# A fused transformer block on one NeuronCore: four rounds of 3, 4, 4 and 5 k tiles in place of 4, 4, 4 and 4, idle products on TensorE ahead of w_mod's last rows, casts ahead of affine halves

## Chip, cores, metric

One core of one Trainium2 chip (trn2). The metric is the device time of one execution in microseconds; a kernel's time is the median of its runs.

## What is computed

The reference is one layer of an adaLN-modulated block on x (256 tokens, 2048 channels) in float32:

```python
c_act = silu(c)
mod = c_act @ w_mod + b_mod                  # 2048 -> 6 * 2048
sh1, sc1, g1, sh2, sc2, g2 = split(mod, 6)
h = rmsnorm(x, norm1_w) * (1.0 + sc1) + sh1
x = x + g1 * mixer(h, ...)   # h @ w_in -> q, k, v, z, x/B/C, dt, gates; attention and SSD; w_out
h = rmsnorm(x, norm2_w) * (1.0 + sc2) + sh2
x = x + g2 * swiglu(h, w_ffn_in, w_ffn_out)
return rmsnorm(x, final_norm_w)
```

What matters here is the beginning: h needs sh1 and sc1, and these need the first 4096 columns of all 2048 rows of w_mod (33.5 MB). Only then can h @ w_in begin.

## The kernel before

**Tiles.** Channels lie on the 128 partitions, so x's 2048 channels are 16 k tiles. A weight chunk is four k tiles by 512 columns (1 MB). Every product is made of float32r pieces: ScalarE casts the chunk to `hi`, VectorE makes `lo = w - hi` (`split_chunk`, L339 and L341, two k tiles at a time), the activations are split in the same way (`split_affine`, L309 to L314), and TensorE sums hi x hi, hi x lo and lo x hi. A chunk of kind `cm1` (q, k, B, C) is 48 products of 256 columns (L389 to L392), one of kind `tm` (v) is 24 of 512 columns (L410 to L412).

**Rounds.** So as not to wait for all of w_mod, the first stage goes in rounds over k tiles (`ROUNDS`, L482). A round (loop at L600) loads, for each of w_mod's 16 row blocks kk, the columns of its k tiles of both sections (shift and scale; `mod_load`, 512 KB), and VectorE adds `row * c_act` into `sums` (L632, L634: one operation of 1024 columns). TensorE sums over the partitions with one-column products (`reduce_to`, L610). Round 0 takes some rows straight on TensorE (`ONPE`: both sections of row 11, one of row 15). Columns of sc1 and sh1 follow (L652 to L656), then the affine step makes `hx`, and round r's part of eleven products against w_in (three q, three k, three v, B, C; `first_chunks`) can run. While a round reduces its rows, the chunks of the round before run between pairs of rows; the last two of them (`TAILCH`) run after the columns are there and cover the affine step. Partial sums are added on VectorE (L498); the first product keeps its banks through all rounds.

**Order.** Each engine runs its instructions in the order of the code. `Stream.run` takes a chunk from the queue, splits the next one (load, cast, lo), lets waiting side tasks do a step, and issues the chunk's products. `mod_task` is the lowest of these tasks: it loads the other columns of w_mod (`wm`, 1 MB, L686), and VectorE reduces them in four operations (L695). It has one step per queue entry at most, and its work alternates between a step with a load and an empty one; the chunks of the last round run with a budget that pays for all of it.

**Buffers.** `wraw` has three raw buffers, taken in turn by every chunk and every wm; `wsp` has four of `hi` and four of `lo`, each for two k tiles. `load_chunk`'s DMA is issued on SP, which waits there until the buffer is free; what stands behind it on SP waits too.

**Before the first product.** x is normalized and transposed by TensorE in eight pairs of k tiles (`turn_x`, L471): four pairs early, three behind row 11 (`NEARLY`, L626), the last one behind the first chunk.

Of the kernel before, what the change touches and what calls it, by code (L numbers as in the profile page):

```python
# [152 lines left out]
def tile_hybrid_block(  # L153
# [162 lines left out]

    def load_chunk(ch, parts=1):
        ncol, nk = ch["ncol"], ch["nk"]
        raw = wraw.tile([P, nk, ncol], F32, tag="raw", name=nm("w"), padded_shape=[P, nk, 2048 // nk])
        for k in range(0, nk, nk // parts):  # L320
            r0 = ch["r0"] + k * P
            nc.sync.dma_start(raw[:, k:k + nk // parts, :], ch["w"][
                r0:r0 + nk // parts * P, ch["c0"]:ch["c0"] + ncol].rearrange("(k p) n -> p k n", p=P))
        return raw

    def split_chunk(ch):
        raw = load_chunk(ch)
        got = []
        if ch["kind"] == "dt":

            for k in (0, 8):
# [4 lines left out]
            return got
        for k in range(0, ch["nk"], 2):
            hi = wsp.tile([P, 2, ch["ncol"]], FR, tag="hi", name=nm("hi"), padded_shape=[P, 2, 512])
            A_.copy(hi, raw[:, k:k + 2, :])  # L339
            lo = wsp.tile([P, 2, ch["ncol"]], FR, tag="lo", name=nm("lo"), padded_shape=[P, 2, 512])  # L340
            V.tensor_tensor(lo, raw[:, k:k + 2, :], hi, op=OP.subtract)  # L341
            got += [(hi[:, i, :], lo[:, i, :]) for i in range(2)]
# [161 lines left out]
    def first_chunks(k0, nk):  # L504
        for i, (kind, lst, g, c0) in enumerate(first):
            kept = i < len(kept_banks)
            st.add(dict(kind=kind, w=w_in, r0=k0 * P, c0=c0, k0=k0, nk=nk, first=0 if kept else k0,
                        last=KT - 1 if kept else k0 + nk - 1, act=hact,
                        evacf=add_to(kind, lst, g, 0 if kept else k0), group={}, ncol=512, accs=None,
                        alloc=(lambda i=i: kept_banks[i]) if kept else lambda: [acc() for _ in range(2)],  # L510
                        before=None, after=None, evac=(0.0, 0.0), time=nk / 4))
# [87 lines left out]

    for r, (k0, nk) in enumerate(ROUNDS):  # L600

        nt = nk * P
        sums = modp.tile([P, 2, 512], F32, tag="ma", name=nm("ma"))

        groups = [(misc(), j0, j1, []) for j0, j1 in ([(0, 1), (1, nk)] if r == 0 else [(0, nk)])]

        def reduce_to(group, sec, w, v, stop=False):
            cols, j0, j1, begun = group
            for j in range(j0, j1):
                PE.matmul(cols[:, sec * 4 + j:sec * 4 + j + 1], w[:, j * P:(j + 1) * P], v,  # L610
                          start=not begun, stop=stop, skip_group_check=True)
# [7 lines left out]
        for kk in range(KT):  # L619
            w = mod_load(kk, k0 * P, nt)  # L620
            onpe = ONPE.get(kk, ()) if r == 0 else ()
            for sec in onpe:
                for group in groups:
                    reduce_to(group, sec, w[:, sec, :], cs[:, kk:kk + 1])
            if onpe and kk == min(ONPE):
                for kp in range(NEARLY, KT // 2 - 1):  # L626
                    turn_x(kp, acc)
            rest = [sec for sec in range(2) if sec not in onpe]
            if rest:
                d, w = sums[:, rest[0]:rest[-1] + 1, :nt], w[:, rest[0]:rest[-1] + 1, :]  # L630
                if kk == 0:
                    V.tensor_scalar(d, w, cs[:, kk:kk + 1], None, op0=OP.mult)  # L632
# [16 lines left out]
        for cols, j0, j1, _ in groups:  # L649
            a, b = k0 + j0, k0 + j1  # L650
            if j1 - j0 == 1:
                V.tensor_scalar(sc1[:, a:b], cols[:, 4 + j0:4 + j1], n1T[:, a:b], c1[:, a:b], op0=OP.mult, op1=OP.add)  # L652
            else:
                V.tensor_tensor(sc1[:, a:b], cols[:, 4 + j0:4 + j1], n1T[:, a:b], op=OP.mult)
                V.tensor_tensor(sc1[:, a:b], sc1[:, a:b], c1[:, a:b], op=OP.add)
            V.tensor_tensor(sh1[:, a:b], cols[:, j0:j1], bmT[:, a:b], op=OP.add)  # L656
            for kt in range(a, b):
                split_affine(hx[kt // 2][:, kt % 2, :], xnT[kt // 4][:, kt % 4, :],
                             sc1[:, kt:kt + 1], sh1[:, kt:kt + 1])
                if r == 0:  # L660
                    k = kt - k0
                    if k % 2 == 0:
                        hi, lo = (wsp.tile([P, 2, 512], FR, tag=tag, name=nm(tag)) for tag in ("hi", "lo"))
                    A_.copy(hi[:, k % 2, :], raw[:, k, :])
                    V.tensor_tensor(lo[:, k % 2, :], raw[:, k, :], hi[:, k % 2, :], op=OP.subtract)
# [764 lines left out]
```

## Time and profile before

| | |
|---|---|
| median of 3 runs | 2032.2 us (2031.6 to 2032.31) |
| the profiled execution, device time | 2033.43 us |
| its span in the trace | 2031.7 us |
| granted TensorE clock, mean | 0.996 |
| busy TensorE, VectorE, ScalarE | 98%, 73%, 50% |
| read from HBM | 464.95 MB |

The page gives shares over the whole span. They mix a beginning in which transfers set the pace with a long rest in which TensorE works without a pause, so stretches and single instructions are read beside it. Times within the span count from its start. A transfer's issue and its landing are different things: the issue stands on SP's queue, the landing ends the wait of the engine that needs the data.

### The profile page before, as it was taken

To read this page: it belongs to the slowest core of one execution; us is meant where nothing else is said; L and a number is where in the kernel's file an instruction comes from. 1 tells how busy PE (TensorE), PEld (TensorE's weight loads), DVE (VectorE), ACT (ScalarE), POOL (GpSimd) and SP (SyncE) were. 2 spreads that over 40 slices of the span, in tenths; PEclk is the share of its full clock that TensorE was granted. 3 is DMA by queue.
4 is the path that set the end of the run, shared out by engine and by line. 5 is a ranking of instruction groups with operands and counts; after the bars stand their busy time and mean duration, and the time that the engine had idled before them with its cause. 6 is when DMAs were issued, how large, how long until landed. Compare 5 with 4: busy or idle time off the path is not lost.

```text
span 2031.7 us, 29046 instructions
## 1 busy us (share of the span) xinstructions
PE 1989.4 (98%) x11560; PEld 1746.0 (86%) x11560; DVE 1479.8 (73%) x1957; ACT 1005.9 (50%) x1429; POOL 97.3 (5%) x176
## 2 busy tenths in 40 slices
PE   5999999999999999999999999999999999999998
PEld 4899999888888888888888888888888888888886
DVE  6788887887888888876868787777765555555564
ACT  4443435575666665554544344644444334444443
POOL 1000000001020211100000000100000000000000
PEclk9999999999999999999999999999999999999999
DMA  9998684575565656667777768587865555555553
GB/s 345 348 321 296 229 272 145 175 239 191 192 230 198 228 199 217 223 233 258 274 243 286 274 241 292 182 291 247 283 219 183 194 199 187 198 197 186 199 193 126
DMA packets 218344, 469.02 MB, mean 231 GB/s; under 512 B 10419, under 2 KB 10607, under 8 KB 218208
## 3 DMA queue, kind: packets, MB, share of 16 engines
q1 hardware_dynamic: 214096, 453.61, 64.9%
q0 software_dynamic: 4112, 13.56, 2.1%
q8 instruction: 90, 1.47, 0.3%
q14 instruction: 46, 0.38, 0.1%
HBM read 464.95 MB, written 2.18 MB: 230 GB/s over the span
## 4 chain that ended last, share of the span: by engine, by line
PE 54%; DVE 1%; DMA 1%; issue 0%; ACT 0%; ACTq 0%; DVEq 0%
PE pa L357 25%; PE pa L361 13%; PE pa L410 5%; PE pa L412 5%; PE pa L411 5%; DMA w<-in_w_ssm_proj_dram 1%; PE pb L701 0%; PE pb L720 0%; DVE lo L341 0%; DVE ma L695 0%; DVE s L1298 0%; ACT hi L339 0%; DVE s L1117 0%; DVE t L444 0%; DVE s L1171 0%
## 5 line engine op out<-in xcount | busy, mean ns | idle before, releaser
L341 DVE TENSOR_TENSOR lo<-w,hi 128x1024 fp32r<-128x1024 f32 x662 | 788.8, 1229 | 369.5 <-ACT hi L339 326.3
L339 ACT CAST hi<-w 128x1024 fp32r<-128x1024 f32 x662 | 666.2, 1048 | 550.4 <-PE pa L357 225.1
L357 PE MATMUL pa<-s,hi 128*128 128x512 f32 x3648 | 881.6, 394 | 2.8 <-DVE s L1298 1.2
L357 PEld LDWEIGHTS pa<-s,hi 128*128 128x128 f32 x3648 | 671.2, 189 | 140.8 <-issue 4.4
L361 PEld LDWEIGHTS pa<-s,lo 128*128 128x128 f32 x3648 | 467.7, 191 | 17.8
L361 PE MATMUL pa<-s,lo 128*128 128x256 f32 x3648 | 473.1, 283 | 0.0
L410 PE MATMUL pa<-hi,s 128*128 128x512 f32 x576 | 225.9, 392 | 0.0
L411 PE MATMUL pa<-lo,s 128*128 128x512 f32 x576 | 224.3, 389 | 0.1
L412 PE MATMUL pa<-hi,s 128*128 128x512 f32 x576 | 224.2, 389 | 0.0
L695 DVE SCALAR_TENSOR_TENSOR ma<-wm,cs,ma 128x512 f32<-128x512 f32 x240 | 164.3, 744 | 3.2 <-DMA wm<-in_w_mod_dram 3.2
L443 ACT COPY t<-pa 128x256 f32<-128x256 f32 x160 | 59.6, 372 | 182.9 <-PE pa L361 168.6
L389 PE MATMUL pa<-s,hi 128*128 128x256 f32 x512 | 148.4, 290 | 0.0
L392 PE MATMUL pa<-s,lo 128*128 128x256 f32 x512 | 145.8, 285 | 0.2 <-DVE lo L341 0.2
L391 PE MATMUL pa<-s,hi 128*128 128x256 f32 x512 | 145.6, 284 | 0.0
L410 PEld LDWEIGHTS pa<-hi,s 128*128 128x128 f32 x576 | 108.1, 188 | 23.5 <-ACT s L496 0.6
L411 PEld LDWEIGHTS pa<-lo,s 128*128 128x128 f32 x576 | 108.2, 188 | 23.3 <-DVE lo L341 0.6
L412 PEld LDWEIGHTS pa<-hi,s 128*128 128x128 f32 x576 | 108.1, 188 | 22.8
L389 PEld LDWEIGHTS pa<-s,hi 128*128 128x128 f32 x512 | 99.1, 194 | 2.3 <-ACT s L496 1.3
L391 PEld LDWEIGHTS pa<-s,hi 128*128 128x128 f32 x512 | 99.2, 194 | 1.0 <-issue 1.0
L392 PEld LDWEIGHTS pa<-s,lo 128*128 128x128 f32 x512 | 99.0, 193 | 0.6 <-DVE lo L341 0.6
L444 DVE TENSOR_TENSOR s<-pa,t 128x256 f32<-128x256 f32 x128 | 53.1, 422 | 52.9 <-ACT t L443 48.6
L634 DVE SCALAR_TENSOR_TENSOR ma<-s,cs,ma 128x1024 f32<-128x1024 f32 (+1 forms) x59 | 75.0, 1272 | 2.5 <-DMA s<-in_w_mod_dram 1.1
(243 smaller groups left out, 1119.5 us busy)
## 6 DMA issues: line engine op xcount, KB each, us to landing
w<-in_w_in_dram SPq DMA_DIRECT2D x147, 1024.0 KB, 5.1
w<-in_w_ffn_in_dram SPq DMA_DIRECT2D x88, 1024.0 KB, 5.0
wm<-in_w_mod_dram SPq DMA_DIRECT2D x64, 1024.0 KB, 5.1
w<-in_w_ffn_out_dram SPq DMA_DIRECT2D x44, 1024.0 KB, 5.1
s<-in_w_mod_dram SPq DMA_DIRECT2D x64, 512.0 KB, 10.2
w<-in_w_ssm_proj_dram SPq DMA_DIRECT2D x32, 1024.0 KB, 5.2
w<-in_w_out_dram SPq DMA_DIRECT2D x16, 1024.0 KB, 5.3
s<-acd POOLq DMA_DIRECT2D x16, 512.0 KB, 4.8
```

Source lines behind the costliest of these rows:

```text
L339: A_.copy(hi, raw[:, k:k + 2, :])
L341: V.tensor_tensor(lo, raw[:, k:k + 2, :], hi, op=OP.subtract)
L357: PE.matmul(accs[n], parts[k][0][:, n * P:(n + 1) * P], act(k0 + k), start=(k0 + k == first), stop=False, skip_group_check=True)
L361: PE.matmul(accs[n][:, :S], parts[k][1][:, n * P:(n + 1) * P], act(k0 + k)[:, :S], start=False, stop=(k0 + k == last), skip_group_check=True)
L389: PE.matmul(o, w1, a[:, :S], start=(kk == first and n % 2 == 0), stop=False, skip_group_check=True)
L391: PE.matmul(o, w1, a[:, S:], start=False, stop=False, skip_group_check=True)
L392: PE.matmul(o, w2, a[:, :S], start=False, stop=(kk == last), skip_group_check=True)
L410: PE.matmul(o, xh, hi, start=(kk == first), stop=False)
L411: PE.matmul(o, xh, lo, start=False, stop=False)
L412: PE.matmul(o, xl, hi, start=False, stop=(kk == last))
L634: V.scalar_tensor_tensor(d, w, cs[:, kk:kk + 1], d, op0=OP.mult, op1=OP.add)
L695: V.scalar_tensor_tensor(a[:, i, :], w[:, 2 * k + i, :], cs[:, kk:kk + 1], a[:, i, :], op0=OP.mult, op1=OP.add)
```

## The change

Four things change in the first stage.

1. `ROUNDS` is (0, 3), (3, 4), (7, 4), (11, 5). Round 0 loads 384 columns per section and row, its chunks have three k tiles. The last round has five: the first four as before, the fifth with a tile `w5` (four small loads for four rows), an accumulator `sums5` and one more VectorE operation per row. Its eleven products become 22 queue entries, each a chunk of four k tiles and one of one. A chunk of one k tile takes a whole raw buffer, a whole hi buffer and a whole lo buffer.
2. `ONPE` takes one section of row 11 in place of both.
3. All four remaining transposes stand behind row 11, and behind them six idle products of 128 columns whose result nobody reads (`IDLE`).
4. In round 0 the cast of a k tile stands ahead of its affine half on ScalarE.

```diff
+        per = -(-nk // parts)
+        for k in range(0, nk, per):
+            m = min(per, nk - k)
...
-    NEARLY, ONPE = 4, {11: (0, 1), 15: (1,)}
+    IDLE = 6
+    NEARLY, ONPE = 4, {11: (0,), 15: (1,)}
...
-    ROUNDS = [(0, 4), (4, 4), (8, 4), (12, 4)]
+    ROUNDS = [(0, 3), (3, 4), (7, 4), (11, 5)]
...
-            st.add(dict(kind=kind, w=w_in, r0=k0 * P, c0=c0, k0=k0, nk=nk, first=0 if kept else k0,
+            group = {}
+            for ka in range(k0, k0 + nk, 4):
+                m = min(4, k0 + nk - ka)
+                st.add(dict(kind=kind, w=w_in, r0=ka * P, c0=c0, k0=ka, nk=m, first=0 if kept else k0,
...
-        nt = nk * P
+        nt = min(nk, 4) * P
+        sums5 = t2(2 * P).rearrange("p (a b) -> p a b", a=2) if nk > 4 else None
...
+            if nk > 4 and kk % 4 == 0:
+                w5 = s4(2, 512).rearrange("p a (b c) -> p (a b) c", c=P).rearrange("p (k s) c -> p k s c", k=4)
+                for k in range(4):
+                    nc.sync.dma_start(w5[:, k, :, :], w_mod_s[
+                        (kk + k) * P:(kk + k + 1) * P, 0:2, (k0 + 4) * P:(k0 + 5) * P])
+            if nk > 4:
+                w = w5[:, kk % 4, :, :]
...
+                    V.scalar_tensor_tensor(sums5, w, cs[:, kk:kk + 1], sums5, op0=OP.mult, op1=OP.add)
...
-                for kp in range(NEARLY, KT // 2 - 1):
+                for kp in range(NEARLY, KT // 2):
                     turn_x(kp, acc)
+                idle = misc()
+                for _ in range(IDLE):
+                    PE.matmul(idle[:, :P], ident, ones, start=True, stop=True)
...
-            ch["after"] = lambda: turn_x(KT // 2 - 1)
...
-                split_affine(hx[kt // 2][:, kt % 2, :], xnT[kt // 4][:, kt % 4, :],
-                             sc1[:, kt:kt + 1], sh1[:, kt:kt + 1])
                 if r == 0:
...
                     A_.copy(hi[:, k % 2, :], raw[:, k, :])
+                split_affine(hx[kt // 2][:, kt % 2, :], xnT[kt // 4][:, kt % 4, :],
+                             sc1[:, kt:kt + 1], sh1[:, kt:kt + 1])
```

In the rows of the order below, a name's number is the buffer's; line numbers of the kernel after lie a little higher. TensorE ahead of the first product, before (`s_97` and `s_101` are x, `cs` is c_act, `s_279` row 15 of w_mod, `ma` the sums):

```order
L471 MATMUL pa_264<-ident,s_97 128x128
L471 MATMUL pa_264<-ident,s_101 128x128
L610 MATMUL pb_207<-cs,s_279 128x1
L610 MATMUL pb_208<-cs,s_279 128x1 x3
L610 MATMUL pb_207<-ones,ma_206 128x1 x2
L610 MATMUL pb_208<-ones,ma_206 128x1 x6
L389 MATMUL pa_181<-s_173,hi_303 128x256
```

The same place on TensorE after (`s_288` is row 15):

```order
L475 MATMUL pa_265<-ident,s_97 128x128
L475 MATMUL pa_265<-ident,s_101 128x128
L657 MATMUL pb_271<-ones,ident 128x128 x6
L624 MATMUL pb_207<-cs,s_288 128x1
L624 MATMUL pb_208<-cs,s_288 128x1 x2
L624 MATMUL pb_207<-ones,ma_206 128x1 x2
L624 MATMUL pb_208<-ones,ma_206 128x1 x4
L392 MATMUL pa_181<-s_173,hi_305 128x256
```

Six idle products have come in between the transposes and row 15, and the one-column products are fewer, as the second group has two k tiles instead of three.

VectorE while the last round's rows are reduced, one step, before (`s_2106` and `s_2109` are two rows, `lo` a chunk of the round before):

```order
L634 SCALAR_TENSOR_TENSOR ma_1765<-s_2106,cs,ma_1765 128x1024
L634 SCALAR_TENSOR_TENSOR ma_1765<-s_2109,cs,ma_1765 128x1024
L341 TENSOR_TENSOR lo_2116<-w_2112,hi_2114 128x1024
L341 TENSOR_TENSOR lo_2120<-w_2112,hi_2118 128x1024
L498 TENSOR_TENSOR s_736<-pa_2122,s_736 128x512
L498 TENSOR_TENSOR s_736<-pa_2123,s_736 128x512
```

The same step on VectorE after (`s_1937` is w5, `w_1645` is sums5):

```order
L645 SCALAR_TENSOR_TENSOR w_1645<-s_1937,cs,w_1645 128x256
L664 SCALAR_TENSOR_TENSOR ma_1646<-s_2013,cs,ma_1646 128x1024
L645 SCALAR_TENSOR_TENSOR w_1645<-s_1937,cs,w_1645 128x256
L664 SCALAR_TENSOR_TENSOR ma_1646<-s_2017,cs,ma_1646 128x1024
L344 TENSOR_TENSOR lo_2023<-w_2020,hi_2022 128x1024
L344 TENSOR_TENSOR lo_2027<-w_2020,hi_2026 128x1024
L502 TENSOR_TENSOR s_664<-pa_2030,s_664 128x512
L502 TENSOR_TENSOR s_664<-pa_2031,s_664 128x512
```

Two operations of 256 columns stand in each step more than before.

SP at the beginning of the last round's chunks, before (`w` are chunks, `wm` the loads of `mod_task`):

```order
L322 DMA w_2459<-in_w_in_dram 128x4x512
L686 DMA wm_2469<-in_w_mod_dram 128x2x1024
L322 DMA w_2526<-in_w_in_dram 128x4x512
L322 DMA w_2588<-in_w_in_dram 128x4x512
L686 DMA wm_2598<-in_w_mod_dram 128x2x1024
L322 DMA w_2656<-in_w_in_dram 128x4x512
L322 DMA w_2718<-in_w_in_dram 128x4x512
L686 DMA wm_2728<-in_w_mod_dram 128x2x1024
```

The same place on SP after:

```order
L324 DMA w_2314<-in_w_in_dram 128x4x512
L324 DMA w_2384<-in_w_in_dram 128x512
L720 DMA wm_2390<-in_w_mod_dram 128x2x1024
L324 DMA w_2444<-in_w_in_dram 128x4x512
L324 DMA w_2469<-in_w_in_dram 128x512
L720 DMA wm_2475<-in_w_mod_dram 128x2x1024
L324 DMA w_2531<-in_w_in_dram 128x4x512
L324 DMA w_2555<-in_w_in_dram 128x512
L720 DMA wm_2561<-in_w_mod_dram 128x2x1024
```

One wm used to stand behind every two chunks of four k tiles; now one stands behind every pair of a four-tile and a one-tile chunk, for the first eight pairs.

## Rows read from the trace of the kernel before

**Rows 1.** Page, part 1: busy time of each engine, its share, instructions

```profile
PE 1989.4 (98%) x11560; PEld 1746.0 (86%) x11560; DVE 1479.8 (73%) x1957; ACT 1005.9 (50%) x1429; POOL 97.3 (5%) x176
```

**Rows 2.** Stretches: length, busy PE, PEld, DVE, ACT, POOL; clock, DMA share, GB/s

```profile
0.00:40.00 40.00, 15.01 (x68) 14.09 (x68) 21.29 (x30) 17.10 (x25) 8.12 (x21) 1.00 0.97 334
...
167.00:234.00 67.00, 66.86 (x483) 62.65 (x483) 60.06 (x70) 25.13 (x28) 0.00 (x0) 1.00 0.83 287
234.00:302.00 68.00, 68.00 (x504) 65.17 (x504) 56.63 (x77) 27.98 (x31) 0.00 (x0) 1.00 0.74 251
```

**Rows 3.** Waits of TensorE: total us, times, longest

```profile
PE pb L610 <- DMA s<-in_w_mod_dram: 7.1, 1, 7.1
```

**Rows 4.** Timeline of TensorE to the first chunk's end: start, us, engine, line

```profile
29.37 3.54 PE L610 MATMUL pb<-cs,s 128*128 128x1 f32 x16 [7.14 <-DMA s<-in_w_mod_dram]
32.78 2.80 PE L471 MATMUL pa<-ident,s 128*128 128x128 f32 x12
35.37 1.71 PE L610 MATMUL pb<-cs,s 128*128 128x1 f32 x8
36.94 3.55 PE L610 MATMUL pb<-ones,ma 128*128 128x1 f32 x16
40.35 0.56 PE L389 MATMUL pa<-s,hi 128*128 128x256 f32 x1
...
44.34 0.39 PE L389 MATMUL pa<-s,hi 128*128 128x256 f32 x1
...
47.92 0.28 PE L392 MATMUL pa<-s,lo 128*128 128x256 f32 x1
48.04 0.60 PE L471 MATMUL pb<-ident,s 128*128 128x128 f32 x4
```

**Rows 5.** Transfers, 0 to 120 us, 40 slices of 3 us

```profile
GB/s 18 193 353 327 359 361 386 388 386 388 386 387 386 386 388 384 385 387 386 388 386 387 387 386 387 389 354 258 141 306 320 262 405 388 382 102 366 392 391 382
```

**Rows 6.** Timeline of VectorE ahead of the first product

```profile
37.97 0.28 DVE L652 TENSOR_SCALAR sc<-pb,v,c 128x1 f32<-128x1 f32 x1 [2.48 <-PE pb L610]
...
39.55 0.69 DVE L665 TENSOR_TENSOR lo<-w,hi 128x512 fp32r<-128x512 f32 x1
```

**Rows 7.** Timeline of VectorE while the last round's rows are reduced

```profile
192.40 0.69 DVE L498 TENSOR_TENSOR s<-pa,s 128x512 f32<-128x512 f32 x1 [2.03 <-PE pa L392]
...
204.97 2.60 DVE L634 SCALAR_TENSOR_TENSOR ma<-s,cs,ma 128x1024 f32<-128x1024 f32 x2
...
209.75 1.28 DVE L498 TENSOR_TENSOR s<-pa,s 128x512 f32<-128x512 f32 x2
210.95 2.59 DVE L634 SCALAR_TENSOR_TENSOR ma<-s,cs,ma 128x1024 f32<-128x1024 f32 x2
```

**Rows 8.** Timeline of TensorE at the last step of that stretch

```profile
225.94 0.39 PE L412 MATMUL pa<-hi,s 128*128 128x512 f32 x1
226.17 0.39 PE L410 MATMUL pa<-hi,s 128*128 128x512 f32 x1
226.69 0.50 PE L411 MATMUL pa<-lo,s 128*128 128x512 f32 x1
```

**Rows 9.** Groups of VectorE, 45 to 300 us: busy us, mean ns, idle before

```profile
L313 DVE TENSOR_SCALAR t<-s,sc,sh 128x256 f32<-128x256 f32 x12 | 4.9, 408 | 0.1
```

**Rows 10.** Last round: ScalarE, VectorE, SP in time; median us from issue to landing

```profile
251.80 2.00 ACT L339 CAST hi<-w 128x1024 fp32r<-128x1024 f32 x2
252.88 2.36 DVE L341 TENSOR_TENSOR lo<-w,hi 128x1024 fp32r<-128x1024 f32 x2 [2.11 <-ACT hi L339]
259.96 2.73 DVE L695 SCALAR_TENSOR_TENSOR ma<-wm,cs,ma 128x512 f32<-128x512 f32 x4
263.81 2.35 DVE L341 TENSOR_TENSOR lo<-w,hi 128x1024 fp32r<-128x1024 f32 x2
266.18 5.77 SPq L322 DMA_DIRECT2D w<-in_w_in_dram  x2
...
w<-in_w_in_dram SPq DMA_DIRECT2D x10, 1024.0 KB, 5.0
```

More of the change, by code (lines that the diff above doesn't have):

```diff
@@ L318, in load_chunk @@
         ncol, nk = ch["ncol"], ch["nk"]
-        raw = wraw.tile([P, nk, ncol], F32, tag="raw", name=nm("w"), padded_shape=[P, nk, 2048 // nk])
-        for k in range(0, nk, nk // parts):
+        raw = wraw.tile([P, nk, ncol], F32, tag="raw", name=nm("w"), padded_shape=[P, max(nk, 4), 2048 // max(nk, 4)])
+        per = -(-nk // parts)
+        for k in range(0, nk, per):
+            m = min(per, nk - k)
             r0 = ch["r0"] + k * P
-            nc.sync.dma_start(raw[:, k:k + nk // parts, :], ch["w"][
-                r0:r0 + nk // parts * P, ch["c0"]:ch["c0"] + ncol].rearrange("(k p) n -> p k n", p=P))
+            nc.sync.dma_start(raw[:, k:k + m, :], ch["w"][
+                r0:r0 + m * P, ch["c0"]:ch["c0"] + ncol].rearrange("(k p) n -> p k n", p=P))
         return raw
@@ L337, in split_chunk @@
         for k in range(0, ch["nk"], 2):
[L338 to L342, printed above, removed]
+            m = min(2, ch["nk"] - k)
+            hi, lo = (wsp.tile([P, m, ch["ncol"]], FR, tag=tag, name=nm(tag), padded_shape=[P, m, 1024 // m])
+                      for tag in ("hi", "lo"))
+            A_.copy(hi, raw[:, k:k + m, :])
+            V.tensor_tensor(lo, raw[:, k:k + m, :], hi, op=OP.subtract)
+            got += [(hi[:, i, :], lo[:, i, :]) for i in range(m)]
         return got
@@ L506, in first_chunks @@
             kept = i < len(kept_banks)
-            st.add(dict(kind=kind, w=w_in, r0=k0 * P, c0=c0, k0=k0, nk=nk, first=0 if kept else k0,
[L508 to L511, printed above, removed]
+            group = {}
+            for ka in range(k0, k0 + nk, 4):
+                m = min(4, k0 + nk - ka)
+                st.add(dict(kind=kind, w=w_in, r0=ka * P, c0=c0, k0=ka, nk=m, first=0 if kept else k0,
+                            last=KT - 1 if kept else k0 + nk - 1, act=hact,
+                            evacf=add_to(kind, lst, g, 0 if kept else k0), group=group, ncol=512, accs=None,
+                            alloc=(lambda i=i: kept_banks[i]) if kept else lambda group=group: group.get("accs") or [
+                                acc() for _ in range(2)],
+                            before=None, after=None, evac=(0.0, 0.0), time=m / 4))
     TAILCH, BIASR = 2, 2
@@ L609, in reduce_to @@
             for j in range(j0, j1):
-                PE.matmul(cols[:, sec * 4 + j:sec * 4 + j + 1], w[:, j * P:(j + 1) * P], v,
+                if j == 4:
+                    w, j = sums5[:, sec, :], 0
+                    o = cols[:, 8 + sec:9 + sec]
+                else:
+                    o = cols[:, sec * 4 + j:sec * 4 + j + 1]
+                PE.matmul(o, w[:, j * P:(j + 1) * P], v,
                           start=not begun, stop=stop, skip_group_check=True)
@@ L619, in tile_hybrid_block @@
         for kk in range(KT):
+            if nk > 4 and kk % 4 == 0:
[5 more added lines that the diff above has]
+                w = w5[:, kk % 4, :, :]
+                if kk == 0:
+                    V.tensor_scalar(sums5, w, cs[:, kk:kk + 1], None, op0=OP.mult)
+                else:
+                    V.scalar_tensor_tensor(sums5, w, cs[:, kk:kk + 1], sums5, op0=OP.mult, op1=OP.add)
             w = mod_load(kk, k0 * P, nt)
@@ L648, in tile_hybrid_block @@
                 reduce_to(group, sec, sums[:, sec, :], ones[:, 0:1], True)
[L649 to L652, printed above, removed]
+        ready = [(cols, j0, 4 + j0, k0 + j0, k0 + min(j1, 4)) for cols, j0, j1, _ in groups]
+        if nk > 4:
+            ready.append((groups[0][0], 8, 9, k0 + 4, k0 + 5))
+        for cols, jh, jc, a, b in ready:
+            ps_h, ps_c = cols[:, jh:jh + b - a], cols[:, jc:jc + b - a]
+            if b - a == 1:
+                V.tensor_scalar(sc1[:, a:b], ps_c, n1T[:, a:b], c1[:, a:b], op0=OP.mult, op1=OP.add)
             else:
-                V.tensor_tensor(sc1[:, a:b], cols[:, 4 + j0:4 + j1], n1T[:, a:b], op=OP.mult)
+                V.tensor_tensor(sc1[:, a:b], ps_c, n1T[:, a:b], op=OP.mult)
                 V.tensor_tensor(sc1[:, a:b], sc1[:, a:b], c1[:, a:b], op=OP.add)
-            V.tensor_tensor(sh1[:, a:b], cols[:, j0:j1], bmT[:, a:b], op=OP.add)
+            V.tensor_tensor(sh1[:, a:b], ps_h, bmT[:, a:b], op=OP.add)
             for kt in range(a, b):
-                split_affine(hx[kt // 2][:, kt % 2, :], xnT[kt // 4][:, kt % 4, :],
-                             sc1[:, kt:kt + 1], sh1[:, kt:kt + 1])
                 if r == 0:
@@ L664, in tile_hybrid_block @@
                     A_.copy(hi[:, k % 2, :], raw[:, k, :])
+                split_affine(hx[kt // 2][:, kt % 2, :], xnT[kt // 4][:, kt % 4, :],
+                             sc1[:, kt:kt + 1], sh1[:, kt:kt + 1])
+                if r == 0:
                     V.tensor_tensor(lo[:, k % 2, :], raw[:, k, :], hi[:, k % 2, :], op=OP.subtract)
@@ L668, in tile_hybrid_block @@
             first_chunks(k0, nk)
-        st.run(PHASE0, len(first))
+        st.run(PHASE0, len(first) * -(-nk // 4))
     mods_done = []
@@ L1093, in start_attention @@
             tk[f"att{i}"] = spawn(attention(i), 0)
-    st.queue[-3]["after"] = start_attention
-    for i, k in ((-2, "B"), (-1, "C")):
-        st.queue[i]["after"] = lambda i=i, k=k: start_conv(k, 0, ubc[i])
+    per = -(-ROUNDS[-1][1] // 4)
+    st.queue[-1 - 2 * per]["after"] = start_attention
+    for i, k in enumerate("BC"):
+        st.queue[-1 - (1 - i) * per]["after"] = lambda i=i, k=k: start_conv(k, 0, ubc[i])
     st.add(dict(kind="dt", w=w_in, r0=0, c0=DT0, k0=0, nk=KT, first=0, last=KT - 1, act=hact, evacf=dt_evac,
```

## The prediction

> **What bounds the kernel now.** I read the page's engine line first [rows 1]: TensorE is busy for 98% of the span. The stretches [rows 2] place the rest: nearly all of its idle time lies ahead of 40 us, and from there to the end of the four rounds (302 us) it is busy throughout. The list of its waits says the same: the one long wait on a transfer is for w_mod's row 11, 7.1 us [rows 3]. A busy TensorE can still be fed late, since overlapping products hide small gaps, so I then read distances between starts. From 29.37 us TensorE works without a gap through 16 + 12 + 8 + 16 records to the first real product at 40.35 [rows 4]: 52 records in 10.98 us, 0.211 us each. Products keep that slow pace until 44.3; at 47.92 they start 0.12 us apart [rows 4]. Those are the two clock levels, 1.2 and 2.4 GHz. From then on a chunk of four k tiles of q or k costs 48 x 0.12 = 5.76 us, and one of v 24 x 0.23 = 5.46 us (0.2275 each, 225.94 to 226.17 [rows 8]). So two things move the end: when the first chunk is through, and every wait of TensorE that the change creates up to 302 us. Work shifted between rounds moves it not at all, as the products are equally many.
>
> The third view is VectorE in the stretch that reduces the last round's w_mod rows: it is busy 60.1 of 67 us [rows 2]. A step (two rows 2.60, a chunk's lo halves 2.35, two adds 1.28, overlapping) repeats after 210.95 - 204.97 = 5.98 us [rows 7, 10], against TensorE's 5.76. VectorE still waited 2.03 us for TensorE at 192.40 [rows 7]; at 226.17 TensorE's next product starts 0.52 us later instead of 0.23 [rows 8]. The reserve is used up exactly there.
>
> **The change, part by part.** The sum is made against the profiled execution, 2033.4 us, which is 1.2 us over the median of the runs, 2032.2; I put the difference on the median.
>
> *Start.* Round 0's w_mod rows fall from 524 to 393 KB. At the 387 GB/s that the transfers sustain [rows 5] a row takes 1.02 us instead of 1.36; the twelfth row then lands 4.1 us earlier, and TensorE starts at 25.3. Its records are again 52: 6 for row 11, 16 transposes, 12 for six idle products (an fp32 product shows as two records, as L610 does), 6 and 12. At the slow pace the first group's columns are ready after 44 of them, at 34.6. The trace shows one rise of the clock, 4 us after full-width products begin; it does not show whether transposes and idle products bring it. I take a rise near their end, 31.5, which halves the rest: columns at 33.1. From columns to chunk end VectorE decides: first lo 2.4 us later (37.97 to 40.24, [rows 6]), second 2.3 later, third 1.4, and 11 products x 0.12 behind it: 7.4 us, so 40.5. Before, the chunk ended at 48.04, or 46.6 without the 12 products that go to later rounds. Gain 6.1, less 0.5 because the second chunk's lo stands behind two rows (1.6 us of waiting; before 1.2, with transposes that now come early): **-5.6**. Bounds: no rise ahead of the products -3.9; a rise at the first transposes -7.1; if a 1.5 KB piece costs what a 2 KB piece does, about -2. I take -5.6, since 6 us of transposes and idle products stand there in one piece. Casts ahead of affine halves are inside the 2.4; ScalarE has nothing else to do there.
>
> *Round 0.* A step loads two rows and a 0.79 MB chunk, 4.7 us at 387 GB/s; TensorE needs 36 x 0.12 = 4.3 us and 0.3 of bias and vector work. The second chunk's data is there some 6 us ahead, and that lead covers it: nothing. But its last two chunks are shorter, and they hide the four affine tiles: VectorE reaches the first lo half of the last one after 0.2 + 4 x 0.85 + 0.5 + 1.1 = 5.3 us, TensorE after 4.5: **+0.8**. The second round begins with that much less lead: **+0.2**.
>
> *Reducing the last round's rows.* The fifth tile adds one 256-column operation per row. Nothing shows it; the nearest row is the 256-column L313, 0.41 us [rows 9]. A step grows by 0.82, to 6.80. The first two steps' 1.6 us go into the 2.03 us wait, the other six make 4.9, of which 0.3 fits: **+4.6** (3.5 to 5). The four small loads per group only add issues on SP ahead of rows that lie a step ahead.
>
> *Last affine.* A fifth tile puts 1.2 us on VectorE ahead of the last chunk's lo, which has 0.3 us to spare, and four more slow records: **+1.4**.
>
> *Last round.* This is the largest term. Each chunk takes one of three raw buffers, and SP may issue a load only when the lo half that reads the buffer's last content is done: 263.81 + 2.35 = 266.16, issue at 266.18 [rows 10]. Now a round has 22 chunks instead of 11, and the order shows one w_mod load (wm) behind each of the first eight pairs of a four-tile and a one-tile chunk. Three buffers then turn once per pair, so a four-tile load waits for the lo half of the four-tile chunk right before it. The loop is landing 5.0, then from the start of the cast to the end of lo 3.44 (251.80 to 255.24), and 0.1 between [rows 10]: 8.55 us. TensorE needs 60 x 0.12 = 7.2 us a pair (6.8 for v). Before, a buffer turned once in two chunks, 11.5 us, and the same loop was hidden. The second pair's lo is ready 7.5 us after the round's start (TensorE gives its hi buffer back after 42 products, 5.0, then a cast and a lo half follow), seven loops make 59.9, the ninth pair is through 5.2 later: 72.6, against 6 x 7.2 + 3 x 6.8 = 63.6 without waits. **+9.0**, bounds 7 and 11 for loops of 8.3 and 8.9. The wm rows themselves (2.73 a pair) fit, as VectorE has 6.8 us of work in 8.55; the two pairs behind the eighth find buffers earlier.
>
> The Trainium skill, page "DMA: Bandwidth & Descriptors", section "Anatomy of one DMA — SWDGE (gpsimd) path", speaks against this cut: a transfer has a fixed part of about 2.0 us and then bytes / 436 GB/s, so smaller loads do not shorten the loop in proportion. By its fit a 1 MB load would take an estimated 4.4 us, the loop 7.95, the term 4.8 and the time 2038.4. The trace's 5.0 for loads issued by SP decides here.
>
> Sum: -5.6 + 0.8 + 0.2 + 4.6 + 1.4 + 9.0 = **+10.4 us**, 2042.6. Its own bounds, with all terms at one end, are 2038 and 2047.
>
> **Rivals.** *The last round's loop is hidden.* For it: VectorE is idle for 11 of the 68 us from 234 to 302 [rows 2]. Against it: the order leaves no other buffer, and idle time of VectorE does not bring a load earlier. It holds if the loop is under 7.2 us: 9.0 falls away, 2033.6, no change. *Faster: the reserves carry both.* Place: the last reduction and the last round. Were lo halves far enough ahead there that both the 4.9 us and the loop vanish, only the start and the affine terms would stand: 2032.2 - 5.6 + 2.4 = 2029, and 2027.5 with the start's upper bound. It decides from a reserve of 5 us at 192 us; the trace has 2.03 there and none at 226. *The start gives little.* If the smaller pieces land no sooner and the clock rises only with the products, -2 stands for -5.6: 2046.2. For it: no row shows a 1.5 KB piece.
>
> **How the numbers follow.** Forecast 0.72, loop hidden 0.11, faster 0.08, start gives little 0.09. A measurement of this kernel tells about 0.2%, 4 us, from no change, so from 2028.1 to 2036.3 is the same. The forecast and the weak start lie above; a small part of the forecast's low end with the hidden loop lies inside: faster 0.08, same 0.14, slower 0.78. The range 2034 to 2048 takes in the forecast's bounds, the weak start and the upper half of the hidden loop; the faster case and that case's lower half stay out, some 0.15.
>
> **What would show it.** Right: the first chunk of 36 products ends near 40.5 us; VectorE runs without a gap through the last reductions in steps of 6.8; in the last round SP's four-tile loads are 8.5 us apart, each right behind a lo half, and TensorE waits for lo or hi about 1.4 us in each of six or seven pairs; the round's end lies some 10 us later. Wrong: loads issued ahead of the lo half before them, pairs 7.2 us apart, or a step of VectorE below 6.3 us; and for the start, row 11 still landing at 29 us.

## The result and the profile after

The changed kernel takes 2044.37 us (median of 6 runs, 2043.21 to 2045.06), the kernel before 2032.26 us in the same session: ratio 1.0057, 95% interval 1.0046 to 1.0067. It is slower by 12 us where 10.4 were forecast. Of the profiled executions the spans are 2042.3 and 2031.7 us, 10.6 apart; the ledger below is made against these.

Part 1 of the page after, the answer to [rows 1], looks the same as before: TensorE is busy for 98%. The share hides what happened; the stretches and the waits show it. Here are stretches near those of [rows 2] (length, busy PE, PEld, DVE, ACT, POOL, then granted clock, DMA share, GB/s), against 66.86 of 67 and 68.00 of 68 us busy there. They are stretches of time and not of equal work: in the changed kernel the last round's rows are reduced from 145 to 216 us, and its chunks run from 229 us on.

```profile
167.00:234.00 67.00, 63.33 (x446) 58.07 (x445) 61.91 (x86) 21.28 (x24) 0.00 (x0) 1.00 0.72 244
234.00:313.00 79.00, 71.76 (x484) 64.26 (x483) 58.36 (x78) 25.19 (x30) 0.00 (x0) 1.00 0.79 260
```

What TensorE waited for from 229 to 313 us (total us, times, longest), all of it data of its own chunks, where before nothing was listed:

```profile
PE pa L395 <- DVE lo L344: 3.7, 8, 0.8
PE pa L414 <- DVE lo L344: 2.3, 3, 0.8
PE pa L413 <- ACT hi L343: 0.9, 2, 0.5
```

These waits count only the time in which nothing overlaps. The full loss ("lost" below) is the distance between starts of consecutive TensorE records beyond the usual one of the same shape (0.12 us for 256 columns, 0.23 for 512), summed over a stretch that ends at the same piece of work in both traces:

| piece of work | lost before | lost after | difference | forecast |
|---|---|---|---|---|
| start to the second chunk's end (55.02 and 45.60), less 96 and 72 products of 0.12 | 43.5 | 37.0 | -6.5 | -5.6 |
| rest of round 0 | 1.2 | 1.2 | 0.0 | 0 |
| second round's sums, last chunks of round 0, second round (to 166 and 145 us) | 3.3 | 4.8 | +1.5 | +1.0 |
| reduction of the last round's rows (to 232 and 216) | 2.2 | 6.0 | +3.8 | +4.6 |
| last affine step, with four more one-column records (to 245 and 229) | 0.0 | 2.3 | +2.3 | +1.4 |
| last round (to 302 and 313) | 0.0 | 11.8 | +11.7 | +9.0 |
| behind it, to 400 us | | | +0.9 | 0 |
| one stall near 870 us | 3.7 | 0.0 | -3.7 | 0 |
| rest | | | +0.6 | 0 |

The start, TensorE in time (start, us, engine, line), the answer to [rows 4]:

```profile
25.91 1.10 PE L624 MATMUL pb<-cs,s 128*128 128x1 f32 x6 [3.57 <-DVE ma L664]
26.88 3.30 PE L475 MATMUL pa<-ident,s 128*128 128x128 f32 x16
30.01 1.50 PE L657 MATMUL pb<-ones,ident 128*128 128x128 f32 x12
...
31.94 1.48 PE L624 MATMUL pb<-ones,ma 128*128 128x1 f32 x12
33.66 0.39 PE L392 MATMUL pa<-s,hi 128*128 128x256 f32 x1 [0.24 <-ACT s L311]
...
41.34 0.39 PE L395 MATMUL pa<-s,lo 128*128 128x256 f32 x1 [1.42 <-DVE lo L344]
```

Row 11 is used at 25.9 instead of 29.4, the first product starts at 33.66 instead of 40.35. The 12 idle records take 1.34 us (to 31.35), 0.112 each: the clock was at its upper level before they began (granted clock 0.50 from 28 to 29 us, 1.00 from 30 us on). At 41.34 the second chunk waits 1.42 us for its lo half.

VectorE, one step of the last reduction, the answer to [rows 7]:

```profile
192.29 0.47 DVE L645 SCALAR_TENSOR_TENSOR w<-s,cs,w 128x256 f32<-128x256 f32 x1
192.68 1.28 DVE L664 SCALAR_TENSOR_TENSOR ma<-s,cs,ma 128x1024 f32<-128x1024 f32 x1
193.88 0.48 DVE L645 SCALAR_TENSOR_TENSOR w<-s,cs,w 128x256 f32<-128x256 f32 x1
194.27 1.28 DVE L664 SCALAR_TENSOR_TENSOR ma<-s,cs,ma 128x1024 f32<-128x1024 f32 x1
195.47 2.35 DVE L344 TENSOR_TENSOR lo<-w,hi 128x1024 fp32r<-128x1024 f32 x2
197.74 1.28 DVE L502 TENSOR_TENSOR s<-pa,s 128x512 f32<-128x512 f32 x2
198.94 0.48 DVE L645 SCALAR_TENSOR_TENSOR w<-s,cs,w 128x256 f32<-128x256 f32 x1
```

No idle time, and the step repeats after 198.94 - 192.29 = 6.65 us. The fifth tile's operation moves the next start by 0.39 us, not 0.41.

The last round, ScalarE, VectorE and SP in time, the answer to [rows 10]:

```profile
245.75 2.36 DVE L344 TENSOR_TENSOR lo<-w,hi 128x1024 fp32r<-128x1024 f32 x2 [2.91 <-ACT hi L343]
248.14 2.14 SPq L324 DMA_DIRECT2D w<-in_w_in_dram  x2
252.59 0.37 SPq L720 DMA_DIRECT2D wm<-in_w_mod_dram  x1
253.39 2.51 ACT L343 CAST hi<-w 128x1024 fp32r<-128x1024 f32 x3 [6.21 <-DMA w<-in_w_in_dram]
254.48 2.36 DVE L344 TENSOR_TENSOR lo<-w,hi 128x1024 fp32r<-128x1024 f32 x2 [1.91 <-ACT hi L343]
256.87 2.14 SPq L324 DMA_DIRECT2D w<-in_w_in_dram  x2
```

One turn of the loop is seen whole: lo ends at 248.1, SP issues the next four-tile load at 248.14, ScalarE waits 6.21 us and casts at 253.39, lo ends at 256.84, and the next load goes out at 256.87. The loads stand at 238.41, 248.14, 256.87, 265.81, 274.54, 283.46 and 292.11, 8.95 us apart on average, and TensorE needs 7.2.

### The profile page after: what moved, and what is told of

Same layout as the page of the kernel before. It is cut to its first block, busy times and chain, and to the rows that moved or that the text cites. A ratio compares the mean times of both kernels' runs of the same rounds, so it can differ in the third digit from the quotient of the medians.

```text
span 2042.3 us, 29174 instructions
## 1 busy us (share of the span) xinstructions
PE 1991.7 (98%) x11560; PEld 1742.1 (85%) x11560; DVE 1485.2 (73%) x1986; ACT 1007.3 (49%) x1439; POOL 97.9 (5%) x176
## 4 chain that ended last, share of the span: by engine, by line
PE 79%; DVE 5%; DMA 4%; issue 2%; ACT 1%; POOL 1%; SPq 0%; ACTq 0%; DVEq 0%; POOLq 0%
PE pa L360 39%; PE pa L364 20%; PE pa L414 5%; PE pa L415 5%; PE pa L413 5%; DVE lo L344 3%; DMA w<-in_w_in_dram 2%; ACT hi L343 1%; DMA s<-in_w_mod_dram 1%; PE pb L1021 1%; PE pb L735 1%; DMA w<-in_w_ssm_proj_dram 1%; POOL nt L301 0%; PE pb L1039 0%; DVE ma L729 0%
## 5 line engine op out<-in xcount | busy, mean ns | idle before, releaser
L344 DVE TENSOR_TENSOR lo<-w,hi 128x1024 fp32r<-128x1024 f32 (+1 forms) x673 | 791.6, 1213 | 385.7 <-ACT hi L343 338.7
L343 ACT CAST hi<-w 128x1024 fp32r<-128x1024 f32 (+1 forms) x673 | 668.0, 1035 | 593.4 <-PE pa L360 229.2
L395 PEld LDWEIGHTS pa<-s,lo 128*128 128x128 f32 x512 | 98.6, 193 | 10.4 <-DVE lo L344 9.6
L664 DVE SCALAR_TENSOR_TENSOR ma<-s,cs,ma 128x1024 f32<-128x1024 f32 (+2 forms) x60 | 72.1, 1201 | 1.1
```

What stands on the lines that cost most here:

```text
L343: A_.copy(hi, raw[:, k:k + m, :])
L344: V.tensor_tensor(lo, raw[:, k:k + m, :], hi, op=OP.subtract)
L395: PE.matmul(o, w2, a[:, :S], start=False, stop=(kk == last), skip_group_check=True)
```

## Experiments

Each kernel was timed in turn with the kernel before, which took 2032.6 to 2033.1 us in these sessions and 2032.3 us beside the changed kernel. The ratios are against the kernel before; a difference to the changed kernel goes across sessions and is good to about 0.8 us.

### One-tile chunks out of the raw buffers

```diff
-        raw = wraw.tile([P, nk, ncol], F32, tag="raw", ...)
+        raw = s4(1, 512) if nk == 1 else wraw.tile([P, nk, ncol], F32, tag="raw", ...)
```

> The changed kernel, but the raw data of a one-tile chunk goes into a free slot buffer, so that the three raw buffers are taken by four-tile chunks and w_mod loads alone. Theory (raw-buffer loop): in the changed kernel's trace the four-tile loads of the last round are issued 8.7 us apart (238.4, 248.1, 256.9, 265.8, ...), each right behind a lo half, and TensorE loses 11.8 us between 229 and 313 us. With two raw buffers a pair instead of three the loads run a pair ahead, pairs come 7.2 us apart, the loss falls below 2 us and the time to about 2034. Rival (the loss comes from the hi and lo buffers, which a one-tile chunk still takes whole, or from the transfers' rate): pairs stay at 8.7 us and the time at 2044.

Measured: 2031.5 us, ratio 0.9989 (0.9980 to 0.9998), 12.9 us less than the changed kernel. SP in the last round:

```profile
250.27 0.37 SPq L324 DMA_DIRECT2D w<-in_w_in_dram  x1
...
253.02 0.37 SPq L720 DMA_DIRECT2D wm<-in_w_mod_dram  x1
257.47 0.37 SPq L324 DMA_DIRECT2D w<-in_w_in_dram  x1
```

Pairs now come 257.47 - 250.27 = 7.20 us apart, TensorE's own pace, with no wait of TensorE from 215 to 300 us. Hi and lo buffers were left as they were, so the raw buffers alone made the loop.

### The fifth tile's sums left out

```diff
-                else:
-                    V.scalar_tensor_tensor(sums5, w, cs[:, kk:kk + 1], sums5, op0=OP.mult, op1=OP.add)
```

> The changed kernel, but the fifth k tile's rows of w_mod are not added up (only the first row is used; the 15 later operations of 256 columns on VectorE are left out, the loads stay). Theory (VectorE's extra operations set the last reduction): a step of VectorE falls from 6.65 to about 5.9 us, TensorE's loss from 145 to 216 us falls from 6.0 to about 2.2 us, and the time by 3.8 us to 2040.5. Rival (the loss comes from the four small loads on SP or from the data landing late): the loss stays and the time is 2044.

Measured: 2040.0 us (1.0034, 1.0022 to 1.0047), 4.4 less. VectorE's step is back at 202.07 - 196.09 = 5.98 us, as before, and the stretch to the round's sums is 4 us shorter:

```profile
196.09 2.59 DVE L662 SCALAR_TENSOR_TENSOR ma<-s,cs,ma 128x1024 f32<-128x1024 f32 x2
...
202.07 2.59 DVE L662 SCALAR_TENSOR_TENSOR ma<-s,cs,ma 128x1024 f32<-128x1024 f32 x2
```

The four small loads a group stayed in; TensorE's waits in this stretch come to 0.2 us, so no loss is left that could be theirs.

### Rounds of four, with the other start edits

```diff
-    ROUNDS = [(0, 3), (3, 4), (7, 4), (11, 5)]
+    ROUNDS = [(0, 4), (4, 4), (8, 4), (12, 4)]
```

> The changed kernel with rounds of four k tiles each, as before; the transposes, the idle products, one section of row 11 on TensorE and the casts ahead of affine halves stay. Theory (the first chunk's gain of 7.1 us has two sources, smaller rows and a shorter, faster queue of TensorE behind row 11; the losses all come from the fifth tile): row 11 lands at 29.2 us again, the first product starts at about 37.3 instead of 40.35, the first chunk ends near 44.7 instead of 48.0, nothing is lost later, 2029 us. Rival (without smaller rows the start gains nothing, since row 15 lands at 34.7 and TensorE has as many slow records behind it as before): 2032.

Measured: 2032.3 us (0.9999, 0.9989 to 1.0008): the rival. TensorE at the start:

```profile
29.49 1.83 PE L624 MATMUL pb<-cs,s 128*128 128x1 f32 x8 [7.03 <-DMA s<-in_w_mod_dram]
31.19 3.65 PE L475 MATMUL pa<-ident,s 128*128 128x128 f32 x16
34.64 2.56 PE L657 MATMUL pb<-ones,ident 128*128 128x128 f32 x12
37.04 0.95 PE L624 MATMUL pb<-cs,s 128*128 128x1 f32 x8
37.85 1.93 PE L624 MATMUL pb<-ones,ma 128*128 128x1 f32 x16
39.64 0.36 PE L392 MATMUL pa<-s,hi 128*128 128x256 f32 x1
```

Here the idle records run at the lower level, 37.04 - 34.64 = 2.4 us for 12, and stand on the path. The granted clock rises at 36.9, the one-column records then start 0.108 us apart, and from 40.3 to 43.7 it is at the lower level again. The second chunk ends 0.2 us earlier than before. My theory, which gave the shorter queue 3 us, fell for this kernel. The part of the smaller rows in the 6.5 us is then 6.3 (54.81 - 45.60, less 24 products of 0.12); between the two kernels without idle products (r4444i0h and idle0) it is 52.70 - 45.28 - 2.88 = 4.5 us, since in rounds of four the idle products themselves cost some 2 us.

### Without idle products

```diff
-    IDLE = 6
+    IDLE = 0
```

> The changed kernel without the six idle products. Theory (the clock is up before they begin: the 16 transposes took 3.1 us, 0.196 each, the 12 idle records 0.112 each): TensorE stands idle from 30.0 to 31.35 instead, the clock stays up, the first chunk ends at 39.5 as before and the time is 2044. Rival (the idle products lift or hold the clock): the first chunk's products begin at 0.21 us each, up to 18 of them, the chunk ends 1 to 2 us later, 2045.5.

Measured: 2041.45 us (1.0037, 1.0024 to 1.0050), 2.9 less than with them: neither theory. The clock fell for the first chunk (granted clock 0.5 from 34.3 to 37.8), which took 6.68 us instead of 5.85, as the rival says. But the second chunk ended at 45.28 instead of 45.60, since it waits for its lo half in either case. A further 0.6 us came at 80 to 90 us, where the clock did not fall this time (below), and 1.9 in the last round, where the four-tile loads landed after 5.0 to 5.15 us instead of 5.0 to 6.2. No row shows how the idle products would reach that far. The timed runs were faster too, so it is more than the scatter of one profiled execution; why stays open.

### The fifth tile's sums on GpSimd

```diff
-                    V.tensor_scalar(sums5, w, cs[:, kk:kk + 1], None, op0=OP.mult)
+                    nc.gpsimd.tensor_scalar(sums5, w, cs[:, kk:kk + 1], None, op0=OP.mult)
...
-                    V.scalar_tensor_tensor(sums5, w, cs[:, kk:kk + 1], sums5, op0=OP.mult, op1=OP.add)
+                    p5 = t2(2 * P).rearrange("p (a b) -> p a b", a=2)
+                    nc.gpsimd.tensor_scalar(p5, w, cs[:, kk:kk + 1], None, op0=OP.mult)
+                    nc.gpsimd.tensor_tensor(sums5, sums5, p5, op=OP.add)
```

(on top of the slots edit)

> The changed kernel with one-tile raw data in slots and the fifth tile's rows added up on GpSimd (two operations a row) instead of VectorE. Theory (the two losses are separate and add): the 3.7 us that leaving these sums out brought come on top of the 12.9 of the slots, 2027.8. Rival (GpSimd beside VectorE is slow, 0.58 us and more where it takes 0.19 alone, so its 62 operations last longer than the reduction, or VectorE slows down beside them): the last reduction waits for GpSimd, 2031.5 or more.

Measured: 2032.8 us (0.9997, 0.9988 to 1.0007), no better than the slots alone. GpSimd and VectorE beside each other:

```profile
178.92 2.91 DVE L666 SCALAR_TENSOR_TENSOR ma<-s,cs,ma 128x1024 f32<-128x1024 f32 x2
181.75 2.89 DVE L344 TENSOR_TENSOR lo<-w,hi 128x1024 fp32r<-128x1024 f32 x2
182.41 2.94 POOL L646 TENSOR_SCALAR w<-s,cs 128x256 f32<-128x256 f32 x1
185.77 2.91 DVE L666 SCALAR_TENSOR_TENSOR ma<-s,cs,ma 128x1024 f32<-128x1024 f32 x2
```

VectorE's step is 185.77 - 178.92 = 6.85 us, longer than with the fifth tile's operations in it (6.65): two rows take 2.9 instead of 2.6, two lo halves 2.9 instead of 2.35, as long as GpSimd runs. The operation left VectorE, and its price stayed. It is the second half of the rival, VectorE slowing down; GpSimd itself was busy for only 43 of the some 70 us of the reduction.

### The second chunk ahead of the second round's rows

```diff
         for kk in range(KT):
+            if r == 1 and kk == 0:
+                st.queue[1]["parts"] = st.split(st.queue[1])
```

(on top of the GpSimd edit; `early0` without idle products)

> As both5, and the second chunk of round 0 is loaded and split ahead of the second round's first two rows. Theory (with the clock up, the start is set by the second chunk's lo halves, which stand behind two rows on VectorE: TensorE waits 1.4 us at 39.76): the second chunk ends at 43.9 instead of 45.6, 1.6 us less than both5, 2026.2. Rival (the rows that now land later cost the same in round 0, which is bound by transfers): as both5.

> As early, without the six idle products. Without them the changed kernel's clock did not fall at 80.9 us (1.5 us less there, 0.9 of it given back to a wait for lo at 89), and its first chunk was 0.8 us slower. Theory (the first chunk now counts, since the second one no longer waits for its lo): 0.8 us more at the start, up to 0.9 less at 81 to 90, together the same as early within 0.5. Rival (the first chunk's clock is hidden behind the transfers of round 0 anyway): 0.6 to 1.5 us less than early.

Measured: 2032.0 us (0.9997, 0.9987 to 1.0006) and 2031.0 us (0.9988, 0.9979 to 0.9998). The second chunk no longer waited (4.41 us instead of 6.1), but both first chunks ran partly at the low clock (6.6 us instead of 5.85), with idle products and without: second chunk's ends at 46.1 and 45.3 us, against 45.3 in both5. So neither reached its theory, and they settle nothing on the lo wait. They do show that the idle products do not hold the clock: in `early` it fell again behind them, from 35.9 to 39.3 us.

### Five tiles in the third round

```diff
-    ROUNDS = [(0, 3), (3, 4), (7, 4), (11, 5)]
+    ROUNDS = [(0, 3), (3, 4), (7, 5), (12, 4)]
```

> The changed kernel with rounds of 3, 4, 5 and 4 tiles, so that the round of five is the third one, beside whose chunks no w_mod side load is issued. Theory (the loop of the last round needs the side load as third user of the raw buffers; VectorE's loss belongs to the reduction of five tiles wherever it is): no wait for lo beyond 1 us a pair in the round of five and none in the last round, 11.8 us less than the changed kernel; VectorE's steps of 6.65 us and a loss of 3 to 5 us stay in the reduction of the third round; the stall near 870 us may come back (4.5 us). 2033 to 2037. Rival (one-tile chunks alone make the loop, by the hi and lo buffers that they take whole): pairs of the round of five at 8.7 us, 2044.

Measured: 2029.6 us (0.9985, 0.9975 to 0.9995), 15 us less than the changed kernel, with all one-tile chunks in raw buffers. No wm is issued beside the round of five, and TensorE waits there for nothing. Nor did VectorE's loss follow the fifth tile in full. Its step, and all of TensorE's waits from 85 to 149 us:

```profile
117.29 0.48 DVE L645 SCALAR_TENSOR_TENSOR w<-s,cs,w 128x256 f32<-128x256 f32 x1
...
123.94 0.48 DVE L645 SCALAR_TENSOR_TENSOR w<-s,cs,w 128x256 f32<-128x256 f32 x1
```

```profile
PE pa L414 <- DVE lo L344: 0.4, 1, 0.4
```

The step is 6.65 us again, but the loss in this reduction is 1 us over that of the changed kernel's third round, not 3.8. TensorE has side work in this stretch (turning the bias tables), so that its own step is 6.2 us here and not 5.76 (two chunks' worth of products from 103.18 to 115.55), and the lead of the lo halves lasts nearly to the end; that this slack is what saves the rest is argued from these two paces, not tested by itself. The stall near 870 us came back, with a wait of 2.0 us.

### The stall near 870 us

The ledger's -3.7 us belongs to a wait of the kernel before, far behind the change. VectorE, GpSimd and TensorE there (13 GpSimd operations make one chain), and the stretch behind it with the granted clock (0.57):

```profile
867.23 2.73 DVE L695 SCALAR_TENSOR_TENSOR ma<-wm,cs,ma 128x512 f32<-128x512 f32 x4
867.40 0.62 POOL L294 TENSOR_SCALAR ni<-nv 128x2 int32<-128x2 int32 x1 [11.42 <-DVE nv L292]
868.11 0.58 POOL L299 TENSOR_TENSOR nt<-ni 128x2 f32<-128x2 f32 x1
868.77 0.58 POOL L300 TENSOR_TENSOR nt<-nt,nv 128x2 f32<-128x2 f32 x1
869.44 0.57 POOL L301 TENSOR_SCALAR nt<-nt 128x2 f32<-128x2 f32 x1
870.10 0.20 POOL L302 TENSOR_TENSOR ni<-ni,nt 128x2 f32<-128x2 f32 x1
...
873.07 0.70 PE L1037 MATMUL pb<-t,ones 128*128 128x256 f32 x2 [2.03 <-DVE t L1034]
```

```profile
874.00:878.00 4.00, 4.00 (x13) 3.11 (x12) 4.00 (x5) 0.00 (x0) 0.00 (x0) 0.57 0.11 41
```

Beside a wm step of VectorE GpSimd's operations take 0.57 to 0.62 us and start as far apart as VectorE's (0.68 us); alone they take 0.2. TensorE waits 2.03 us for the chain, and its clock then falls. The test holds that wm step back in the kernel before:

```diff
+        st.hold = g == 7
         rs = pool_rstd(ps[:, :2], 512)
         yield "D", 0.4, 0.0
+        st.hold = False
```

> The kernel before (not the changed one), with one w_mod step of the side task held back while the last gated-norm chain of x and z (eighth group) runs. The trace of before loses 4.5 us near 870 us that the changed kernel and the one with one-tile chunks in slots don't lose: GpSimd's 13 small operations take 5.1 us there (0.58 to 0.62 each for the first four, beside VectorE's w_mod step, 0.19 to 0.20 without), TensorE waits 2.0 us for the result, and its granted clock then falls to 0.76. Theory (the w_mod step beside the chain makes it late; in the changed kernel that step stands elsewhere by chance): the chain takes 3.5 us, the wait and the slow stretch go, 2028.5 us. Rival (the chain is late for another reason, the loss stays or moves to the next step): 2032.7.

Measured: 2028.85 us (0.9981, 0.9972 to 0.9990), 3.9 less. GpSimd's chain and TensorE in that kernel:

```profile
867.68 0.19 POOL L294 TENSOR_SCALAR ni<-nv 128x2 int32<-128x2 int32 x1 [11.43 <-DVE nv L292]
...
870.99 0.20 POOL L302 TENSOR_TENSOR ni<-ni,nt 128x2 f32<-128x2 f32 x1
...
871.76 0.70 PE L1039 MATMUL pb<-t,ones 128*128 128x256 f32 x2 [0.44 <-DVE t L1036]
```

The clock stays up from 874 to 878 us. In the changed kernel 16 one-column sums of w_mod stand on TensorE ahead of this product and no wm step beside the chain, as the last round's 22 queue entries had moved the side task on; so it has no such wait. The other kernels bear this out: where the last round has four tiles (rounds4444, rounds3454) the 2.0 us wait is there, and where it has five (slots5, noadd5, idle0, both5) it is not. That is luck of the order, and it hides 3.7 us of what the rounds cost.

### Combinations

`slots5i0` is the slots edit without idle products, `r4444i0h` is rounds of four without idle products and with the hold, `r3454h` is the third round of five with the hold.

> As slots5 (one-tile raw data in slots, the fifth tile's sums on VectorE), without the six idle products. Theory (what idle0 showed against the changed kernel, 0.3 us at the second chunk and 0.9 to 1.5 at 80 us where the clock then does not fall, holds here too): 2030.2. Rival (where the clock falls hangs on less than a microsecond of shift, it falls elsewhere): as slots5, 2031.5.

> A candidate: rounds of four tiles each and no idle products, the other start edits (all transposes and one section of row 11 on TensorE, casts ahead of affine halves), and the w_mod step held back beside the last gated-norm chain, as in hold7. Theory (with rounds of four the 12 idle records stood on the path, 2.4 us at the slow pace from 34.64 to 37.04): first product at about 37.2 instead of 39.6, 1 to 2 us less at the end of the second chunk, 2027.2. Rival (row 15 lands at 34.7 and the second chunk's lo halves set the start in any case): as hold7, 2028.9.

> rounds3454 (2029.6 us) with the w_mod step held back beside the last gated-norm chain, as in hold7. Theory (the two are in different stages and add; rounds3454 has the 2.0 us wait and the slow stretch near 870 us again): 3.8 to 4.5 us less, 2025.5. Rival (with other shifts the clock falls somewhere else, or the held step collides with the next one): 2028 to 2029.6.

Measured: 2030.65 us (0.9990, 0.9980 to 0.9999); 2027.96 us (0.9976, 0.9966 to 0.9985); 2027.1 us (0.9973, 0.9963 to 0.9984). The first gains nothing over slots5 (0.9990 against 0.9989): the clock fell at 80.8 us without idle products too, as its rival says. In the second the first product starts at 37.65 us and the second chunk ends 2.3 us earlier than before, as its theory says; but in time it is only 0.9 us ahead of hold7 where 1.7 were expected, and the profiled execution (2030.5 us, the slowest of ten) lost 1.5 again to a slow stretch at 99 us. The third gives 2.5 us over rounds3454 where 4 were expected; it is the fastest kernel here, 5.6 us ahead of the one before and 17 ahead of the changed one, and r4444i0h follows with 4.7 us ahead of the one before.

## Why the prediction was right, and where not

**Forecast and mechanism.** 2042.6 us was forecast, 2044.4 measured. The largest term, the loop of the last round, is shown by its rows and by two kernels that remove it in different ways (slots5, rounds3454). The sign and the size rest on it.

**Last round, +9.0, measured +11.7.** The step that was mis-sized is the loop's first part. I took 5.0 us from issue to landing [rows 10]; here the seven four-tile loads land after 5.0 to 6.2 us, 5.3 on average. The loop is 8.95 us, not 8.55, over seven turns 2.8 us more; the first turn alone, with the landing of 6.2, takes 9.7. Why they land later is open. Loads in flight beside them do not explain it by themselves: in idle0 the same wm and one-tile loads are issued at the same distances, the four-tile loads land after 5.0 to 5.15 us, the loop is 8.64 and the term 9.8. The 7.95 us worked out from the Trainium skill's page "DMA: Bandwidth & Descriptors" is further off than either; the measurement decides against its fit for this loop.

**Reduction, +4.6, measured +3.8.** Mechanism as written, shown by noadd5. The operation costs 0.39 to 0.40 us in the row, so the step is 6.65 and not 6.80.

**Last affine, +1.4, measured +2.3.** I looked at VectorE alone. The chain is longer on ScalarE:

```profile
218.19 2.08 ACT L311 ACTIVATE s<-s,sh,sc 128x256 fp32r<-128x256 f32 x4 [8.20 <-DVE sh L689]
222.09 0.60 ACT L311 ACTIVATE s<-s,sh,sc 128x256 fp32r<-128x256 f32 x1 [1.82 <-DVE sh L689]
222.59 3.87 ACT L343 CAST hi<-w 128x1024 fp32r<-128x1024 f32 x4
```

The fifth tile's affine half waits on ScalarE for its own column, 1.82 us, and the next chunk's cast stands behind it; VectorE then waits 0.51 us for that cast. From the columns to the first lo it is 223.66 - 217.72 = 5.9 us, and 4.0 before.

**Start, -5.6, measured -6.5.** The sum came out, its story did not. The clock rose before the idle products and not at their end, and neither rise nor idle products decided: the end of the second chunk is set by its lo half behind two rows on VectorE, in the changed kernel and in idle0 alike. What counts most is the row's size, 4.5 to 6.3 us of it as rounds4444 and r4444i0h show. The 1.00 that [rows 2] print as clock for the first 40 us is no reading: the trace of the kernel before notes no clock ahead of 44.6 us, and the pace of the records, from which I read the level, is half.

**Around 80 us, +1.0, measured +1.5, for another reason.** I priced VectorE's lateness for the last chunk of round 0 (the sum there comes to 5.2 and not 5.3 us, so 0.7). What happened is a fall of the clock, TensorE from 78.64 us on and the stretches with PEclk:

```profile
78.64 1.95 PE L624 MATMUL pb<-ones,ma 128*128 128x1 f32 x16
```

```profile
80.00:82.00 2.00, 2.00 (x15) 2.00 (x15) 1.09 (x5) 0.91 (x2) 0.00 (x0) 0.72 1.01 353
82.00:84.00 2.00, 2.00 (x11) 2.00 (x11) 1.79 (x6) 2.00 (x4) 0.00 (x0) 0.50 1.07 395
```

From 81.1 to 84.3 us products start 0.213 us apart. The lateness that I had priced is there underneath: in idle0, where the clock stayed up, TensorE waits 0.7 us for lo in the second of these chunks, which takes 5.24 us instead of 4.32, about what I had priced. So the mechanism was right, and the measured number is that of the fall, which covers it.

**The missed term.** Nothing ahead of the result looked at the kernel behind 312 us. The change moved the side task's phase, and with it a stall of 3.7 us away. Without this the time would have been near 2048, at the range's end. The terms that I took too small (last round 2.7, affine 0.9, behind it 0.9, around 80 us 0.5) stand against those too large (start 0.9, reduction 0.8) and this gain, and nearly cancel: part of the agreement of the sums is chance.

**The rivals.** "The last round's loop is hidden" and "the reserves carry both" are refuted by the rows of the last round and by noadd5; "the start gives little" by row 11 at 25.9 us.

## What to carry to other kernels

When a load is cut into a large and a small part, count the users of its buffer ring per turn: a third user that is small in bytes can close a loop of landing, cast and last read that two users left open, and a ring of its own for the small part (slots5), or a place without another user (rounds3454), opens it again. Put the odd part of an uneven split where the next stage has slack, and follow the chain behind it on every engine that it crosses. Compare two kernels piece by piece at the same work and not by total alone, as a change of order can move a distant stall.

## What the runs showed of the hardware

**GpSimd and VectorE slow each other.** Operations of two columns take 0.2 us on GpSimd alone and 0.57 to 0.62 beside a VectorE operation that reads two tensors; VectorE's rows of 1024 columns take 1.38 to 1.49 instead of 1.28 us beside GpSimd (both5). The Trainium skill, page "SBUF — State Buffer", section "Who interferes with whom", says that a VectorE instruction with two SBUF inputs contends with a GpSimd instruction that reads SBUF, because its second input comes through the shared read interface, and that the shared port pair is an exclusive lock. The rows at 867 us agree: the starts of GpSimd's first four operations at 867.40, 868.11, 868.77 and 869.44 are as far apart as VectorE's four (2.73 / 4 = 0.68 us).

**The clock falls after runs of one-column products, but not always.** A run of 16 such records (1.7 to 2.2 us for 16 to 20) is followed within 1 us by some 3.2 us at the low level (1.2 GHz, granted clock 0.50) at 80 us in the changed kernel, slots5, noadd5, both5, early0, slots5i0 and rounds3454, and by none in idle0, early and r3454h. The 20 records behind a reduction of five tiles are followed by a fall at 214 to 218 us in slots5, noadd5, both5 and slots5i0 and at 150.5 us in rounds3454, and by none in the changed kernel, idle0, early, early0 and r3454h. In the kernel before no fall follows its runs of 16 at 98, 166 and 232 us. Each fall costs about 1.5 us. TensorE was busy without a gap ahead of the fall at 80 us in the changed kernel (2.00 of 2 us from 78 us on) and of the one at 214 us in noadd5; in slots5 it had idle time there (2.75 of 3 us busy from 210 us on). There are falls of other origin, too, as the one behind the 2.03 us wait near 870 us. What decides between a fall and none is not settled by these runs.
